# A fused two-block transformer kernel: the in-chunk step sums of the mixer, four heads at a time in two-part products

## The chip, the cores and the metric

The kernel runs on one core of one Trainium2 chip. The metric is the device time of one execution in microseconds (us), which is the time of that one core. The profile is one execution recorded by the hardware profiler. Its five compute rows are PE (TensorE matmuls), PEld (TensorE weight loads), DVE (VectorE), ACT (ScalarE) and POOL (GpSimd); SP is the engine that issues most DMAs.

## The reference, cut to what matters

Two transformer blocks are computed for 256 tokens of width 1024, all in 32-bit floats. The second block has a feed-forward part, a mixer and a second feed-forward part. The mixer runs a state-space branch (16 heads of 64, two groups of eight, chunks of 128 tokens) beside an attention branch. Inside a chunk the state-space branch needs, for every head, the sum of the steps between two positions, and its exponential:

```python
a_cum = jnp.cumsum((dt * A).reshape(b, nc, CHUNK, SSD_GROUPS, SSD_HPG), axis=2)
seg = a_cum[:, :, :, None] - a_cum[:, :, None, :]
causal = jnp.tril(jnp.ones((CHUNK, CHUNK), dtype=bool))[None, None, :, :, None, None]
Lmat = jnp.exp(jnp.where(causal, seg, -jnp.inf)).astype(dtype)
cb = jnp.einsum('bclgn,bcsgn->bclsg', Cc, Bc)
y_diag = jnp.einsum('bclsg,bclsgr,bcsgrp->bclgrp', cb, Lmat, xdt)
```

`dt * A` is the step of one position and head. `seg[l, s]` is the sum of the steps at the positions after `s` up to `l`. 16 heads times two chunks make 32 matrices of 128x128.

## The kernel before, in words

**Products.** Almost every large product runs on TensorE as three matmuls of a reduced 32-bit type, called fp32r in the profile. A weight slab is loaded into a tile `raw`, ACT casts its high part `wh` (line 179, or 183 with a gain), and DVE or, for a list of chosen slabs, POOL forms the low part `wl` (lines 180 and 184). `part` (lines 216 to 221) and `by_feature` (lines 240 to 259) then add high by high, high by low and low by high. A few small products are done in full 32 bits with one matmul call each; the profile shows two MATMUL records for each such call.

**Order of the work.** The program writes out the order of every engine's instructions by hand, and each engine works its own queue strictly in that order. The main line is a row of slab products. Side work is written as generators: `start` puts one into a list, and `tick` (lines 92 to 96), called after each piece of a slab product, moves each generator on when the number that it last yielded has been counted down. So a generator's instructions stand in each queue between those of the main line, at the place of its tick. `take` (lines 191 to 204) prepares up to two slabs ahead of the one in use, with five `raw` buffers and five pairs of `wh` and `wl`; a slab's DMA can be issued by SP only when a `raw` buffer is free, which is when its low part has been formed.

**The mixer (from line 1177).** The first product gives the raw steps and the latent queries (`queries`, line 1217), the second the latent keys and values (`keys`, line 1225, which copies the result out of PSUM on ACT, line 1227), the third the B and C inputs (slabs `X["bc"]`, `by_feature` at line 1277). Meanwhile two sorts of generators run. `latent_chain` (line 1207) normalises and transposes the latents: its transposes are PE instructions at line 272, and they read the copy of line 1227. `steps` (line 1191) forms `dt` and `dA`, the step of every position and head (128x32), by a chain of small DVE instructions (lines 338 to 352, then 1197 and 1198). Its second stage is issued in the same tick as the second stage of the second query chain, whose cast is the ACT instruction of line 266 on a tile of 384 columns.

**The state-space part.** `ssd(g)` (line 1377) is a generator that runs beside the products of the gate slabs `X["z", 0]` and `X["z", 1]`, once for each group of eight heads; `inputs(1, ps)` runs beside the first of them and puts its own POOL work (line 1272) into the same queue. Work is cut into four units of four heads (two chunks by two halves). In step s it issues, in this order: for unit s, on POOL, the product of the strict triangle `after` with the steps of four heads (line 1401, a tile `gm` of 128x512, three buffers); for unit s-2, on PE, four products with the inputs (line 1410) and on DVE their sum (line 1412); for unit s-1, on PE, four 32-bit products with `gm` as stationary operand and the triangle `upper` as moving operand of 128 columns (line 1418), on ACT the exponential back into `gm` (line 1419), and on DVE the product with `cb` (line 1420). Steps 1 and 3 have one more 32-bit product of 512 columns each (lines 1424 and 1429). Two ticks pass between steps. Before step 0, POOL forms `xdd` (line 1384).

Of the kernel before, what the change touches and what calls it, by code (L numbers as in the profile page):

```python
# [10 lines left out]
F32R = mybir.dt.float32r  # L11
I32 = mybir.dt.int32
AF = mybir.ActivationFunctionType
OP = mybir.AluOpType
# [4 lines left out]
H = 16  # L19
NEG = -1e30  # L20
EPS = 1e-6
TP = 128
# [6 lines left out]
def kernel(ctx: ExitStack, tc: tile.TileContext, a: dict, out: bass.AP):  # L29
    nc = tc.nc  # L30
    PE, ACT, DVE, POOL = nc.tensor, nc.scalar, nc.vector, nc.gpsimd
# [23 lines left out]
    def mm_ps(shape=(TP, 512)):  # L55
        return psm.tile(list(shape), F32, tag="mm", name="mm")

    BUFS = {"x": 4, "q": 12, "m": 10, "ra": 3, "rb": 6, "pr": 3, "pT": 4, "gm": 3, "rr": 1}

    def sb(tag, shape=(TP, 512), dt=F32, name=None):  # L60
        return s2.tile(list(shape), dt, tag=tag, name=name or tag, bufs=BUFS[tag])

# [3 lines left out]
    def tt(shape, name="t", dt=F32):  # L66
        return tiny.tile(list(shape), dt, tag="t", name=name)

    def f(ap):
        return ap.bitcast(F32)  # L70
# [193 lines left out]
    def split(hi, lo, src):  # L264

        ACT.copy(hi, src)  # L266
        DVE.tensor_tensor(lo, src, f(hi), op=OP.subtract)  # L267
# [70 lines left out]
    def log1p_of(e, shape):  # L338

        z = tt(shape, "z")  # L340
        q = tt(shape, "q")
        DVE.tensor_scalar(q, e, 2.0, None, op0=OP.add)
        DVE.reciprocal(q, q)
        DVE.tensor_tensor(z, e, q, op=OP.mult)
        DVE.tensor_tensor(q, z, z, op=OP.mult)
        r = tt(shape, "r")
        DVE.tensor_scalar(r, q, 1.0 / 17, None, op0=OP.mult)
        for c in (15, 13, 11, 9, 7, 5, 3):
            DVE.scalar_tensor_tensor(out=r, in0=r, scalar=1.0 / c, in1=q, op0=OP.add, op1=OP.mult)
        DVE.scalar_tensor_tensor(out=r, in0=r, scalar=1.0, in1=z, op0=OP.add, op1=OP.mult)  # L350
        DVE.tensor_scalar(r, r, 2.0, None, op0=OP.mult)
        return r
# [116 lines left out]
    upper = const.tile([TP, TP], F32)  # L469
    POOL.affine_select(out=upper, in_=ones, pattern=[[1, TP]], compare_op=OP.is_ge,  # L470
                       fill=0.0, base=0, channel_multiplier=-1)
    after = const.tile([TP, TP], F32)
# [704 lines left out]
    def mixer(xT, chains, gate, next_chain, between):  # L1177
# [4 lines left out]
        dtr = keep.tile([TP, 2, H], F32, name="dtr")  # L1182
        dt = keep.tile([TP, 2, H], F32, name="dt")
        dA = keep.tile([TP, 2, H], F32, name="dA")
        decay = keep.tile([TP, H], F32, name="decay")
        ea = keep.tile([TP, H], F32, name="ea")
        kr = [keep.tile([TP, 32], F32, name=f"kr{t}") for t in range(2)]
# [3 lines left out]
        def steps():  # L1191
            e = tt((TP, 2, H), "dte")
            DVE.scalar_tensor_tensor(out=e, in0=dtr, scalar=-1.0, in1=dtr, op0=OP.mult, op1=OP.min)
            ACT.activation(out=e, in_=e, func=AF.Exp)
            yield 4
            l1 = log1p_of(e, (TP, 2, H))
            DVE.scalar_tensor_tensor(out=dt, in0=dtr, scalar=0.0, in1=l1, op0=OP.max, op1=OP.add)
            DVE.scalar_tensor_tensor(out=dA, in0=dt, scalar=-1.0, in1=a_bc.unsqueeze(1).to_broadcast([TP, 2, H]),
                                     op0=OP.mult, op1=OP.mult)
            yield 8  # L1200
            p = mm_ps((TP, 2, H))
            PE.matmul(p[:, 0, :], lhsT=after, rhs=dA[:, 0, :], start=True, stop=True)
            PE.matmul(p[:, 1, :], lhsT=upper, rhs=dA[:, 1, :], start=True, stop=True)
            ACT.activation(out=decay, in_=p[:, 0, :], func=AF.Exp)
            ACT.activation(out=ea, in_=p[:, 1, :], func=AF.Exp)
# [89 lines left out]
        for hf in range(2):  # L1295
# [9 lines left out]
            for q in range(2):  # L1305
                ps = [mm_ps((TP, 2, 192)) for _ in range(2)]

                def kv_out(t):
                    ACT.mul(ktok[t][:, 2 * q:2 * q + 2, 0:64], ps[t][:, :, 0:64], rk[t])
                    ACT.mul(vt[t][:, 2 * q:2 * q + 2, :], ps[t][:, :, 64:192], rk[t])  # L1310
                    if q == 1:
# [3 lines left out]
                         after=kv_out)  # L1315
# [61 lines left out]
        def ssd(g):  # L1377
            hs = slice(8 * g, 8 * g + 8)
            p = mm_ps((TP, TP))
            PE.transpose(p, bT[:, g, 0:TP], ident)  # L1380
            bt = cbp.tile([TP, TP], F32, tag="cb", name="bt")
            ACT.copy(bt, p)
            xd = sb("rb", name="xdd")
            POOL.tensor_tensor(by_head(xd), by_head(xdt[0][g]), decay[:, hs].unsqueeze(2).to_broadcast([TP, 8, 64]),
                               op=OP.mult)
            cb = []
            for t in range(2):
                p = mm_ps((TP, TP))
                PE.matmul(p, lhsT=bT[:, g, tok(t)], rhs=cT[:, g, tok(t)], start=True, stop=True)
                x = cbp.tile([TP, TP], F32, tag="cb", name="cb")  # L1390
                DVE.tensor_tensor(x, p, upper, op=OP.mult)
                cb.append(x)
            units = [(t, b) for t in range(2) for b in range(2)]
            ms = {}
            prev = None
            for s in range(len(units) + 2):
                if s < len(units):
                    t, b = units[s]
                    h0 = 8 * g + 4 * b
                    m = sb("gm", (TP, 4, TP))  # L1400
                    POOL.tensor_tensor(m, after.unsqueeze(1).to_broadcast([TP, 4, TP]),
                                       dA[:, t, h0:h0 + 4].unsqueeze(2).to_broadcast([TP, 4, TP]), op=OP.mult)
                    ms[s] = m
                if s >= 2:
                    t, b = units[s - 2]
                    m, y = ms.pop(s - 2), xs_tok[t][g]
                    p = mm_ps((TP, 256))
                    for i in range(4):
                        c0 = (4 * b + i) * 64
                        PE.matmul(p[:, i * 64:(i + 1) * 64], lhsT=m[:, i, :], rhs=xdt[t][g][:, c0:c0 + 64],  # L1410
                                  start=True, stop=True)
                    DVE.tensor_tensor(y[:, b * 256:(b + 1) * 256], y[:, b * 256:(b + 1) * 256], p, op=OP.add)
                if 1 <= s <= len(units):
                    t, b = units[s - 1]
                    m = ms[s - 1]
                    p = mm_ps((TP, 4, TP))
                    for i in range(4):
                        PE.matmul(p[:, i, :], lhsT=m[:, i, :], rhs=upper, start=True, stop=True)
                    ACT.activation(out=m, in_=p, func=AF.Exp)
                    DVE.tensor_tensor(m, m, cb[t].unsqueeze(1).to_broadcast([TP, 4, TP]), op=OP.mult)  # L1420
                if s == 1:

                    p = mm_ps()
                    PE.matmul(p, lhsT=bt, rhs=xd, start=True, stop=True)
                    prev = sb("rb", name="prev")
                    ACT.copy(prev, p)
                if s == 3:
                    p = mm_ps()
                    PE.matmul(p, lhsT=cT[:, g, tok(1)], rhs=prev, start=True, stop=True)
                    yo = sb("ra", (TP, 8, 64), name="yo")  # L1430
                    DVE.tensor_tensor(yo, by_head(p), ea[:, hs].unsqueeze(2).to_broadcast([TP, 8, 64]), op=OP.mult)
                    y = xs_tok[1][g]
                    DVE.tensor_tensor(y, y, yo.rearrange("p h d -> p (h d)"), op=OP.add)
                yield 2
# [80 lines left out]
    keep = const  # L1515
# [136 lines left out]
```

## Time and profile before

| | |
|---|---|
| three runs | 1186.57, 1189.31, 1192.03 us (median 1189.31) |
| the profiled execution | 1188.71 us, of which the traced span is 1187.0 us |
| instructions in the trace | 19943 |
| bytes moved by DMA | 243.04 MB, 205 GB/s in the mean |
| granted TensorE clock, mean | 0.996 of full speed |

The profiled execution is 0.60 us below the median of the runs, and 1.71 us of its time lie outside the span. A row of a timeline gives the start in us from the span's start, the duration, the engine, the line, the operation, the tile written and the tiles read, the shape, and in brackets how long the engine had stood idle and what ended it. A row of a table of windows gives, for a stretch, its length, then each engine's busy time with the instruction count, then the granted TensorE clock as a share of full speed, then the DMA share and rate. The durations of neighbouring matmuls overlap; the spacing of their starts is what a matmul costs in a row of them.

### The profile page before, as it was taken

To read this page: it belongs to the slowest core of one execution; us is meant where nothing else is said; L and a number is where in the kernel's file an instruction comes from. 1 tells how busy PE (TensorE), PEld (TensorE's weight loads), DVE (VectorE), ACT (ScalarE), POOL (GpSimd) and SP (SyncE) were. 2 spreads that over 40 slices of the span, in tenths; PEclk is the share of its full clock that TensorE was granted. 3 is DMA by queue.
4 is the path that set the end of the run, shared out by engine and by line. 5 is a ranking of instruction groups with operands and counts; after the bars stand their busy time and mean duration, and the time that the engine had idled before them with its cause. 6 is when DMAs were issued, how large, how long until landed. Compare 5 with 4: busy or idle time off the path is not lost. (4 is left out here: it accounts for less than half of the span.)

```text
span 1187.0 us, 19943 instructions
## 1 busy us (share of the span) xinstructions
PE 1162.7 (98%) x7669; PEld 1047.6 (88%) x7669; DVE 832.5 (70%) x1187; ACT 673.9 (57%) x1148; POOL 250.8 (21%) x226
## 2 busy tenths in 40 slices
PE   8999999999999999999999999999998999999997
PEld 7987989988898799899878999978987887999996
DVE  5664678886666467788687788766776786766445
ACT  6476675565556675566654444535766573444443
POOL 3044202223003502112002121103147400112001
PEclk9999999999999999999999999999999999999999
DMA  8643567887553348799737978843733273777661
GB/s 270 195 142 107 181 219 262 295 287 223 170 174 123 129 151 282 242 308 318 244 133 256 314 274 303 275 154 101 222 92 107 90 268 125 244 222 246 209 193 38
DMA packets 128479, 243.04 MB, mean 205 GB/s; under 512 B 8515, under 2 KB 16612, under 8 KB 128384
## 3 DMA queue, kind: packets, MB, share of 16 engines
q1 hardware_dynamic: 126688, 239.96, 61.4%
q0 software_dynamic: 1376, 1.28, 0.5%
q8 instruction: 60, 0.98, 0.3%
q10 hardware_dynamic: 320, 0.53, 0.1%
q14 instruction: 35, 0.29, 0.1%
HBM read 240.65 MB, written 1.09 MB: 204 GB/s over the span
## 5 line engine op out<-in xcount | busy, mean ns | idle before, releaser
L179 ACT CAST wh<-raw 128x1024 fp32r<-128x1024 f32 (+1 forms) x231 | 237.4, 1041 | 220.3 <-DMA raw<-in_w_down_dram 64.1
L180 DVE TENSOR_TENSOR wl<-raw,wh 128x1024 fp32r<-128x1024 f32 (+1 forms) x201 | 261.5, 1319 | 128.0 <-ACT wh L179 125.9
L252 PE MATMUL mm<-xh,wh 128*128 128x256 f32 x1088 | 308.5, 284 | 0.0
L254 PE MATMUL mm<-xh,wl 128*128 128x256 f32 x1088 | 307.9, 283 | 0.0
L253 PE MATMUL mm<-xl,wh 128*128 128x256 f32 x1088 | 307.9, 283 | 0.0
L184 DVE SCALAR_TENSOR_TENSOR wl<-raw,cols,wh 128x512 fp32r<-128x512 f32 (+1 forms) x270 | 203.8, 806 | 65.2 <-ACT wh L183 65.1
L219 PE MATMUL acc<-wh,mh 128*128 128x512 f32 x524 | 208.0, 397 | 2.4 <-ACT mh L266 2.4
L183 ACT ACTIVATE wh<-raw,cols 128x512 fp32r<-128x512 f32 (+1 forms) x270 | 176.0, 708 | 59.3 <-PE acc L253 20.1
L253 PEld LDWEIGHTS mm<-xl,wh 128*128 128x128 f32 x1088 | 208.8, 192 | 0.8
L252 PEld LDWEIGHTS mm<-xh,wh 128*128 128x128 f32 x1088 | 208.8, 192 | 0.8
L254 PEld LDWEIGHTS mm<-xh,wl 128*128 128x128 f32 x1088 | 208.7, 192 | 0.0
L221 PE MATMUL acc<-wh,ml 128*128 128x512 f32 x524 | 205.1, 391 | 0.0
L220 PE MATMUL acc<-wl,mh 128*128 128x512 f32 x524 | 204.9, 391 | 0.0
L509 POOL PARTITION_ALL_REDUCE ada<-ada x18 | 64.3, 3572 | 338.2 <-DVE ada L504 140.2
L219 PEld LDWEIGHTS acc<-wh,mh 128*128 128x128 f32 x524 | 98.9, 189 | 24.4 <-ACT mh L266 4.0
L221 PEld LDWEIGHTS acc<-wh,ml 128*128 128x128 f32 x524 | 98.6, 188 | 22.5 <-DVE ml L267 1.5
L220 PEld LDWEIGHTS acc<-wl,mh 128*128 128x128 f32 x524 | 99.0, 189 | 19.1 <-DVE wl L180 0.5
L504 DVE SCALAR_TENSOR_TENSOR ada<-raw,c_act,ada 128x512 f32<-128x512 f32 x144 | 107.8, 748 | 3.5 <-DMA raw<-in_w_ada_dram 1.0
L252 PE MATMUL acc<-xh,wh 128*128 128x256 f32 x352 | 102.0, 290 | 0.0
L253 PE MATMUL acc<-xl,wh 128*128 128x256 f32 x352 | 99.5, 283 | 0.0
L254 PE MATMUL acc<-xh,wl 128*128 128x256 f32 x352 | 99.5, 283 | 0.0
L180 POOL TENSOR_TENSOR wl<-raw,wh 128x1024 fp32r<-128x1024 f32 x30 | 71.8, 2396 | 108.9 <-ACT wh L179 103.7
(320 smaller groups left out, 1602.4 us busy)
## 6 DMA issues: line engine op xcount, KB each, us to landing
raw<-in_w_ada_dram SPq DMA_DIRECT2D x72, 512.0 KB, 5.4
raw<-in_w_up_dram SPq DMA_DIRECT2D x64, 512.0 KB, 4.8
raw<-in_w_down_dram SPq DMA_DIRECT2D x64, 512.0 KB, 5.6
raw<-in_ffn_w_gate_dram SPq DMA_DIRECT2D x44, 512.0 KB, 4.9
raw<-in_ffn_w_up_dram SPq DMA_DIRECT2D x44, 512.0 KB, 4.8
raw<-in_ffn_w_down_dram SPq DMA_DIRECT2D x44, 512.0 KB, 4.8
raw<-in_moba_w_qkv_dram SPq DMA_DIRECT2D x23, 512.0 KB, 5.8
raw<-in_w_in_dram SPq DMA_DIRECT2D x20, 512.0 KB, 4.4
```

The source lines that it names most:

```text
L179: ACT.copy(hi, raw)
L180: (POOL if i in on_pool else DVE).tensor_tensor(lo, raw, f(hi), op=OP.subtract)
L183: ACT.mul(hi[:, k], raw[:, k], gain[k])
L184: DVE.scalar_tensor_tensor(out=lo[:, k], in0=raw[:, k], scalar=gain[k], in1=f(hi[:, k]), op0=OP.mult, op1=OP.subtract)
L219: PE.matmul(p, lhsT=xh, rhs=wh, start=first and n == 0, stop=False)
L220: PE.matmul(p, lhsT=xh, rhs=wl, start=False, stop=False)
L221: PE.matmul(p, lhsT=xl, rhs=wh, start=False, stop=last and n == len(ws) - 1)
L252: PE.matmul(o, lhsT=wh[:, c], rhs=xh, start=k == 0 and n % 2 == 0, stop=False)
L253: PE.matmul(o, lhsT=wh[:, c], rhs=xl, start=False, stop=False)
L254: PE.matmul(o, lhsT=wl[:, c], rhs=xh, start=False, stop=k == 7 and n % 2 == 1)
L504: DVE.scalar_tensor_tensor(out=acc, in0=raw[:, i, :], scalar=c_act[:, k:k + 1], in1=acc, op0=OP.mult, op1=OP.add)
L509: POOL.partition_all_reduce(acc, acc, TP, ReduceOp.add)
```

## The change

`dA` is cut into a high and a low part of the type fp32r when it has been formed (ACT copies, DVE subtracts), and ACT copies the triangle `after` into an fp32r tile `after_r`. In `ssd`, POOL now makes two tiles `gx` for each unit, the triangle `upper` times the high parts and the same times the low parts of the steps of four heads, and PE makes one product of 512 columns with each, with `after_r` as stationary operand, summed in PSUM. Before, it was one call of 128 columns for each head. The POOL instructions now come last in the step. The exponential goes to a tile `gm` of its own, with one buffer; `gx` has two.

```diff
-    BUFS = {"x": 4, "q": 12, "m": 10, "ra": 3, "rb": 6, "pr": 3, "pT": 4, "gm": 3, "rr": 1}
+    BUFS = {"x": 4, "q": 12, "m": 10, "ra": 3, "rb": 6, "pr": 3, "pT": 4, "gm": 1, "gx": 2, "rr": 1}
...
         dA = keep.tile([TP, 2, H], F32, name="dA")
+        dAp = [keep.tile([TP, 2, H], F32R, name=f"dA{x}") for x in "hl"]
+        after_r = keep.tile([TP, TP], F32R, name="after_r")
...
             DVE.scalar_tensor_tensor(out=dA, in0=dt, scalar=-1.0, in1=a_bc.unsqueeze(1).to_broadcast([TP, 2, H]),
                                      op0=OP.mult, op1=OP.mult)
+            split(*dAp, dA)
+            ACT.copy(after_r, after)
             yield 8
...
             for s in range(len(units) + 2):
-                if s < len(units):
-                    t, b = units[s]
-                    h0 = 8 * g + 4 * b
-                    m = sb("gm", (TP, 4, TP))
-                    POOL.tensor_tensor(m, after.unsqueeze(1).to_broadcast([TP, 4, TP]),
-                                       dA[:, t, h0:h0 + 4].unsqueeze(2).to_broadcast([TP, 4, TP]), op=OP.mult)
-                    ms[s] = m
                 if s >= 2:
...
                 if 1 <= s <= len(units):
                     t, b = units[s - 1]
-                    m = ms[s - 1]
                     p = mm_ps((TP, 4, TP))
-                    for i in range(4):
-                        PE.matmul(p[:, i, :], lhsT=m[:, i, :], rhs=upper, start=True, stop=True)
+                    for i, m in enumerate(ms[s - 1]):
+                        PE.matmul(p, lhsT=after_r, rhs=m, start=i == 0, stop=i == 1)
+                    m = ms[s - 1] = sb("gm", (TP, 4, TP))
                     ACT.activation(out=m, in_=p, func=AF.Exp)
                     DVE.tensor_tensor(m, m, cb[t].unsqueeze(1).to_broadcast([TP, 4, TP]), op=OP.mult)
+                if s < len(units):
+                    t, b = units[s]
+                    h0 = 8 * g + 4 * b
+
+                    ms[s] = [sb("gx", (TP, 4, TP), F32R) for _ in range(2)]
+                    for m, d in zip(ms[s], dAp):
+                        POOL.tensor_tensor(m, upper.unsqueeze(1).to_broadcast([TP, 4, TP]),
+                                           f(d)[:, t, h0:h0 + 4].unsqueeze(2).to_broadcast([TP, 4, TP]), op=OP.mult)
                 if s == 1:
```

## Rows read from the trace of the kernel before

**Rows 1.** The page, busy time of each engine over the whole span.
```profile
PE 1162.7 (98%) x7669; PEld 1047.6 (88%) x7669; DVE 832.5 (70%) x1187; ACT 673.9 (57%) x1148; POOL 250.8 (21%) x226
```

**Rows 2.** Windows: ten us in the state-space part.
```profile
920.00:930.00 10.00, 8.84 (x51) 6.87 (x49) 5.16 (x9) 5.25 (x10) 7.35 (x8) 1.00 0.20 56
```

**Rows 3.** Timeline of PE: one unit at line 1418 and the matmuls behind it.
```profile
933.22 1.11 PE L1418 MATMUL mm<-upper,gm 128*128 128x128 f32 x8
934.09 0.48 PE L219 MATMUL acc<-wh,xh 128*128 128x512 f32 x1
934.41 0.39 PE L220 MATMUL acc<-wl,xh 128*128 128x512 f32 x1
934.64 0.39 PE L221 MATMUL acc<-wh,xl 128*128 128x512 f32 x1
```

**Rows 4.** Timeline of ACT, around the second stage of `steps`.
```profile
818.55 0.23 ACT L1194 ACTIVATE dte<-dte 128x32 f32<-128x32 f32 x1 [0.21 <-DVE dte L1193]
...
820.98 1.06 ACT L179 CAST wh<-raw 128x1024 fp32r<-128x1024 f32 x1
822.20 1.05 ACT L179 CAST wh<-raw 128x1024 fp32r<-128x1024 f32 x1 [0.16 <-PE acc L221]
823.15 0.39 ACT L1227 COPY ckv<-acc 128x288 f32<-128x288 f32 x1
```

**Rows 5.** Chain that ended last, in order of time, two links on DVE.
```profile
825.55 2.42 DVE r L349
...
829.58 0.20 DVE dA L1198
```

**Rows 6.** Timeline of POOL beside that chain.
```profile
825.51 2.41 POOL L180 TENSOR_TENSOR wl<-raw,wh 128x1024 fp32r<-128x1024 f32 x1
```

**Rows 7.** Timeline of PE: the transposes that read the copy of line 1227.
```profile
827.91 0.38 PE L272 MATMUL mm<-ident,ckv 128*128 128x128 f32 x2
```

**Rows 8.** Timeline of PE: three places at which it stood for over 1.1 us.
```profile
785.50 0.50 PE L219 MATMUL acc<-wh,mh 128*128 128x512 f32 x1 [1.64 <-ACT mh L266]
...
909.81 1.07 PE L1410 MATMUL mm<-xdt,gm 128*128 128x64 f32 x8 [1.21 <-ACT th L1251]
...
926.67 1.16 PE L1418 MATMUL mm<-upper,gm 128*128 128x128 f32 x8 [1.16 <-POOL gm L1401]
```

**Rows 9.** Windows behind the first and the last of these places.
```profile
786.00:788.00 2.00, 2.00 (x6) 1.18 (x6) 1.31 (x3) 1.20 (x2) 0.00 (x0) 0.80 0.73 264
788.00:790.00 2.00, 2.00 (x6) 1.50 (x5) 1.74 (x3) 2.00 (x3) 0.00 (x0) 0.50 0.02 6
790.00:792.00 2.00, 2.00 (x8) 1.56 (x8) 2.00 (x3) 0.08 (x1) 0.00 (x0) 0.84 0.52 147
...
928.00:932.00 4.00, 4.00 (x21) 2.95 (x20) 3.27 (x7) 2.45 (x4) 0.81 (x1) 1.00 0.00 0
```

**Rows 10.** Groups by line and shape: the POOL product of line 1401.
```profile
L1401 POOL TENSOR_TENSOR gm<-after,dA 128x512 f32<-128x512 f32 x8 | 10.1, 1266 | 4.3 <-PE mm L1410 4.3
```

**Rows 11.** Timeline of POOL in the state-space part.
```profile
902.96 2.37 POOL L180 TENSOR_TENSOR wl<-raw,wh 128x1024 fp32r<-128x1024 f32 x1
...
913.54 2.39 POOL L180 TENSOR_TENSOR wl<-raw,wh 128x1024 fp32r<-128x1024 f32 x1 [5.76 <-ACT wh L179]
...
916.73 1.04 POOL L1272 TENSOR_TENSOR xdt<-xs,dt 128x512 f32<-128x512 f32 x1 [0.80 <-ACT xs L1270]
...
918.86 1.49 POOL L1401 TENSOR_TENSOR gm<-after,dA 128x512 f32<-128x512 f32 x1
...
925.58 2.04 POOL L1401 TENSOR_TENSOR gm<-after,dA 128x512 f32<-128x512 f32 x2
```

**Rows 12.** Timeline of DVE beside these POOL instructions.
```profile
904.01 1.87 DVE L1252 SCALAR_TENSOR_TENSOR xf<-th,xf 128x512 f32<-128x512 f32 x1
...
910.79 0.67 DVE L1252 SCALAR_TENSOR_TENSOR xf<-th,xf 128x512 f32<-128x512 f32 x1
...
918.44 1.01 DVE L1420 TENSOR_TENSOR gm<-gm,cb 128x512 f32<-128x512 f32 x1 [1.21 <-ACT gm L1419]
```

## The prediction

> **What bounds the kernel now.** I began with the busy times of the page. PE is busy 98% of the span [rows 1], so whatever shortens PE's own queue is worth its full length, as long as nothing makes PE stand instead. Then I read the stages that the change touches. In the state-space part PE is not full: in one ten-us window it is busy 8.84, while POOL is busy 7.35 [rows 2]. The timeline of PE shows why. At 926.67 PE had stood 1.16 us for the POOL product of line 1401, and at 909.81 it had stood 1.21 us [rows 8]. So the POOL queue sets the pace at one place of this part, and PE at most others. Last I read the stage where `dA` is formed, on ACT, DVE, POOL and PE, since the change puts ACT instructions there.
>
> **PE's saving.** A unit's four 32-bit products start at 933.22, and the next matmul at 934.09: 0.87 us. The first fp32r matmul behind them is followed after 0.32, the next after 0.23, so 0.09 is paid for changing over [rows 3]. The new pair costs two spacings of 512 columns and the same change-over, 0.23 + 0.32 = 0.55, and the matmul behind it no longer pays its 0.09. That is 0.87 + 0.09 - 0.55 = 0.41 us saved in each of eight units, 3.3 us in all.
>
> **The ACT queue at `steps`.** This is the added wait that matters. The copy of the high part of `dA` enters ACT's queue in the tick of the second stage, ahead of the casts that start at 820.98 and 822.20 and of the copy of line 1227 at 823.15 [rows 4]. But `dA` is ready only at 829.78 [rows 5], so ACT stands with all of these behind the copy. The stand shortens one thing. One link of the DVE chain took 2.42 us instead of 0.20, since POOL's low part of a slab ran from 825.51 to 827.92 and it waited for that [rows 5, 6]. That low part needs the cast of 820.98, which is now held, so it cannot run then and the chain ends 2.2 us earlier, at 827.55. ACT then does the new copy (0.23 for 32 columns by line 1194) and that of the triangle (about 0.25, an estimate between 0.23 for 32 and 0.39 for 288 columns), overlapped to 0.3, then the two casts at the spacing of 0.95, which is 1.06 less the overlap of some 0.1, then the copy of line 1227 in 0.39: 827.55 + 0.3 + 1.9 + 0.4 = 830.15. The transposes at 827.91 read that copy [rows 7], and PE cannot pass them. PE comes 2.25 us later. Its bounds are 0, if the chain's other links end earlier than I think, and 4.5, if the chain gains nothing (829.78 + 2.6 less 827.91). I take 2.3, since the link of 2.42 ends with POOL's instruction to 0.05 us. The held slab's low part ends near 831.4 on POOL, before its product at some 832.7, so it costs nothing. Its `raw` buffer comes free 3.4 us later and SP's next loads with it, against 2.3 of PE; the casts of those slabs follow their loads by more than the 1.1 left over, so nothing waits there. The DVE subtraction of the low part, some 0.2 us, lies in this stand.
>
> **The clock behind that stand.** After PE had stood 1.64 us at 785.50, the granted clock fell to 0.50, which is 1.2 of 2.4 GHz, and the three windows behind it read 0.80, 0.50 and 0.84: 2 x (0.20 + 0.50 + 0.16) = 1.7 us of full clock lost. After 1.16 us at 926.67 it stayed at 1.00 [rows 8, 9]. A stand of 2.3 us is nearer to the first. Bounds 0 and 1.7; I take 1.7.
>
> **POOL's second product.** Line 1401 took 1.27 us in the mean and 1.02 where two ran together in 2.04 [rows 10, 11]. The new product has the same shape, and there are 16 instead of 8, so POOL gets 8.2 to 10.1 us more. Where is it covered? At units 1 to 3 of both groups POOL may start when PE has done the pair before, and two products take 2.0 to 2.5, against 6.5 us from pair to pair (926.67 to 933.22) [rows 3, 8]: covered. Formerly it could run two units ahead; that lead is lost, and what is queued behind unit 2 on POOL, the low part at 913.54, waits with it, but POOL stood 5.76 us before that and has room [rows 11]. There are three places without cover.
> - Unit 0 of the first group. POOL went on to line 180 at 902.96, so a second product ends near 904.0, some 1.0 later. PE can do the first of the pair meanwhile and loses some 0.7 us, which the stand of 1.21 at 909.81 takes up again [rows 8, 11].
> - The low part of line 180 at 902.96 moves back by the same 1.0. DVE's line 1252 at 904.01 took 1.87 us there and ended as POOL's instruction did, against 0.67 at 910.79 [rows 11, 12]. If it again waits for the end, the stand at 909.81 grows by 1.0; if DVE gets in ahead, it shrinks by up to 1.2. The two starts lie within 0.1 us of each other, so I take 0 and keep both ends.
> - Unit 0 of the second group. POOL works without a gap from 916.73 on, and the first of the two products at 925.58 ended near 926.6, when PE's stand ended [rows 8, 11]. Into that stretch go a second product of unit 3 (at 918.86 one took 1.49) and one of unit 0 (1.02): 1.3 (between 1.02 and 1.49) + 1.0 = 2.3 us, less 0.4, since the stretch waits for an ACT copy of PE's transposes [rows 11] and PE has unit 1's saving behind it there. POOL is ready at 926.6 + 1.9 = 928.5; only the pair's second matmul is then left, so PE goes on near 928.8, where before its four calls were done 0.9 after 926.67, near 927.6. It is 1.2 later there, and the stand grows from 1.16 to about 3 us, since PE comes 1.2 earlier with three units saved. Bounds: 0.3 later, if both products take their 1.0 beside idle DVE and the stretch begins a us sooner, and 2.1, if it begins no sooner and the products take 1.5.
>
> The last three units save 3 x 0.41 = 1.2, so this part ends where it did: 0. The long stand has again the clock as its price, 1.7 by the row that it is nearer to [rows 8, 9], with 0 as the other end.
>
> Edits at no cost: the one buffer of `gm`, since the products that read it stand ahead of the pair on PE; and `dA` itself at lines 1202 and 1203, read as before.
>
> **A page beside it.** The row of 904.01 shows DVE held to the end of POOL's instruction; that of 918.44 shows the DVE product at 1.01 and a POOL product of 1.49 beside it, both stretched [rows 11, 12]. The Trainium skill, "SBUF — State Buffer", section "SBUF: two separate sides", says that the two engines' shared ports are an exclusive lock held for the whole instruction. By that rule the 0 of the second place would be 1.0 and the sum that much higher; by the row of 918.44, where both got through in part, it stays.
>
> **The sum.** 2.3 for ACT's queue, 1.7 for the clock, 0 for the state-space part (PE's 3.3 is in it) and 1.7 for the clock again make 5.7 us against the profiled execution's 1188.71: 1194.4. The median of the runs is 0.60 above that execution, well inside their own spread of 5.5, so I leave it at **1194.4 us**.
>
> **The rivals.**
> - *The clock stays up.* The stands come as worked out but no low clock follows either. For it speaks that a stand of 1.21 us brought none; against it the one of 1.64. 1188.71 + 2.3 = 1191.0 us. Chance 0.14.
> - *PE's saving is all that shows (faster).* ACT's copy finds `dA` done, or its held work is not waited for, and POOL's product at the second group stays covered. The places are the transposes at 827.91 and the pair at 926.67; the point from which it decides is whether ACT's copy of line 1227 and POOL's second product end before PE arrives. For it: PE is the bound at 98%. Against it: the order of ACT's queue, which is fixed. 1188.71 - 3.3 = 1185.4 us. Chance 0.14.
> - *DVE is held by POOL (slower still).* The place is line 1252 at 904.01. If DVE waits there for the low part that now ends 1.04 later, PE stands at 909.81 for over 2 us, and pays the clock a third time: 1194.4 + 1.0 + 1.7 = 1197.1 us. It decides if POOL takes up its instruction before DVE does. For it the row of 1.87, against it the row of 1.01. By the lock rule of the Trainium skill's page "SBUF — State Buffer" it would come so. Chance 0.20.
> - *The pair is no faster.* If a 512-column product cost as much with these tiles as a 32-bit call of 512 columns, some 0.87 by the same number of columns in a unit, the unit would cost 1.74: 8 x (1.74 - 0.55) = 9.5 us more than in the sum, 1203.9. Against it: every fp32r matmul of 512 columns beside it is 0.23 from the next [rows 3]. Chance 0.02.
>
> **How the numbers follow.** The forecast has a chance of 0.50, with an own range of 1191.5 to 1196.5: it loses part of a low-clock stretch at the lower end, and takes longer POOL instructions at the upper. A measurement of this kernel can tell about 0.5%, 5.9 us, from no change, so faster means under 1183.4 and slower over 1195.3. Slower gets the whole of the third and fourth rivals and somewhat over a quarter of the forecast: 0.20 + 0.02 + 0.14 = 0.36. Faster needs more than all of PE's saving, so it gets 0.04 out of the second rival, for the spread of the runs. The rest, 0.60, is within. The range of 1187.5 to 1198.5 leaves out most of the second rival (0.10), the top of the third (0.06) and the fourth, together under 0.2.
>
> **What would show it.** In the profile after: on ACT a copy of 32 columns at the place of 821, with an idle time of over 6 us before it that DVE ended; the link of the DVE chain back at 0.20; PE idle for about 2.2 us before the transposes of line 272, and a granted clock of 0.50 in the windows behind; 16 POOL products near 1.04 to 1.3 us each; the pair's spacing 0.55 or less; a stand of over 2 us at the first unit of the second group. I am wrong if PE doesn't stand at the transposes, if the clock stays at 1.00 behind both stands, or if the state-space part as a whole gets longer by more than 2 us at full clock.

## The result and the profile after

The changed kernel takes **1196.3 us** (median of 7 runs, 1192.89 to 1198.66) against 1187.91 for the kernel before (7 runs): a ratio of 1.0070, 95% interval 1.0056 to 1.0084. It is slower by 8.4 us, above the 0.5% that was to be told apart; that class had a chance of 0.36, "within" had 0.60. The time lies in the range, 1.9 us above the forecast. The profiled execution took 1197.49, its span is 1195.8. Lines of the changed kernel have other numbers than before: 1251 is now 1255, 1252 is 1256, 1401 is 1424, 1410 is 1407, 1418 is 1414, 1227 is 1231, 1198 is 1200.

The page, busy times of each engine in the kernel after, answers to [rows 1]:

```profile
PE 1164.7 (97%) x7621; PEld 1045.5 (87%) x7621; DVE 833.9 (70%) x1188; ACT 673.0 (56%) x1150; POOL 260.6 (22%) x234
```

PE has 48 matmuls fewer and yet 2.0 us more busy time; its matmuls at half clock take longer (0.63 for 0.39 at 914.74). To see where the time went I cut the span at three PE instructions that the change doesn't touch. First in the kernel before (timeline of PE):

```profile
810.17 0.45 PE L219 MATMUL acc<-qh,xh 128*128 128x400 f32 x1 [1.00 <-ACT xh L266]
...
898.26 0.49 PE L1389 MATMUL mm<-cT,bT 128*128 128x128 f32 x2 [0.91 <-ACT pT L566]
...
988.74 0.60 PE L272 MATMUL mm<-ident,hn 128*128 128x128 f32 x4
```

Then in the kernel after, the same three and every place of the two stretches that matters (timeline of PE):

```profile
809.85 0.45 PE L219 MATMUL acc<-qh,xh 128*128 128x400 f32 x1 [0.99 <-ACT xh L266]
...
828.31 0.44 PE L272 MATMUL mm<-ident,ckv 128*128 128x128 f32 x2 [2.14 <-ACT ckv L1231]
...
899.87 0.49 PE L1393 MATMUL mm<-cT,bT 128*128 128x128 f32 x2 [0.90 <-ACT pT L566]
...
912.31 1.08 PE L1407 MATMUL mm<-xdt,gm 128*128 128x64 f32 x8 [1.75 <-ACT th L1255]
913.20 0.72 PE L1414 MATMUL mm<-gx,after_r 128*128 128x512 f32 x2
913.75 0.39 PE L219 MATMUL acc<-wh,xh 128*128 128x512 f32 x1
...
931.48 0.80 PE L1414 MATMUL mm<-gx,after_r 128*128 128x512 f32 x1 [3.10 <-POOL gx L1424]
...
950.94 1.10 PE L1407 MATMUL mm<-xdt,gm 128*128 128x64 f32 x8 [0.61 <-DVE gm L1417]
...
955.88 1.08 PE L1407 MATMUL mm<-xdt,gm 128*128 128x64 f32 x8 [0.56 <-DVE gm L1417]
...
996.90 0.60 PE L272 MATMUL mm<-ident,hn 128*128 128x128 f32 x4
```

The first stretch, in which `steps` runs, went from 88.09 us (898.26 - 810.17) to 90.02. The second, the state-space part, went from 90.48 to **97.03**. Of the 8.8 us between the spans, 6.55 are in the part that was forecast to gain nothing at full clock and to pay 1.7 for the clock. The pair itself is what it was costed at: 913.20 to 913.75 is 0.55, against 0.87 in [rows 3].

The granted clock behind the stands (windows of the kernel after; the columns are the window, its length, the busy times of PE, PEld, DVE, ACT and POOL, the clock, the DMA share and GB/s):

```profile
828.00:830.00 2.00, 1.69 (x10) 1.69 (x11) 2.00 (x1) 1.94 (x7) 1.92 (x2) 0.68 0.03 8
830.00:832.00 2.00, 2.00 (x12) 2.00 (x12) 2.00 (x14) 1.47 (x5) 1.75 (x4) 0.50 0.44 132
832.00:834.00 2.00, 2.00 (x18) 2.00 (x17) 2.00 (x5) 1.57 (x5) 1.01 (x3) 0.96 0.80 250
...
914.00:916.00 2.00, 2.00 (x6) 1.54 (x5) 1.49 (x3) 1.48 (x2) 2.00 (x2) 0.52 0.74 207
916.00:918.00 2.00, 2.00 (x11) 1.94 (x10) 0.19 (x1) 0.60 (x1) 2.00 (x2) 0.63 0.15 55
...
930.00:932.00 2.00, 0.52 (x1) 0.29 (x1) 0.00 (x0) 0.79 (x2) 2.00 (x3) 0.78 0.23 87
932.00:934.00 2.00, 1.80 (x5) 0.91 (x4) 0.00 (x0) 0.00 (x0) 2.00 (x3) 0.50 0.03 8
934.00:936.00 2.00, 2.00 (x5) 1.25 (x4) 0.98 (x3) 0.00 (x0) 0.42 (x1) 0.50 0.00 0
936.00:938.00 2.00, 2.00 (x8) 1.65 (x7) 1.56 (x3) 0.00 (x0) 0.00 (x0) 0.51 0.00 0
```

With the loss of a window as 2 us times what the clock lacks of 1.00, as the prediction reckoned [rows 9], the three stretches at half clock (1.2 of 2.4 GHz) lose 1.72, 1.70 and 3.42 us. The last is an upper bound, since part of it ran while PE stood.

ACT's queue in the kernel after (timeline of ACT), to be held against [rows 4]:

```profile
825.65 0.22 ACT L266 CAST dAh<-dA 128x32 fp32r<-128x32 f32 x1 [6.47 <-DVE dA L1200]
825.78 0.29 ACT L1203 CAST after_r<-after 128x128 fp32r<-128x128 f32 x1
825.98 1.99 ACT L179 CAST wh<-raw 128x1024 fp32r<-128x1024 f32 x2
827.87 0.39 ACT L1231 COPY ckv<-acc 128x288 f32<-128x288 f32 x1
```

ACT stands 6.47 us for `dA`, then does the two copies and two casts before the copy for which PE has stood 2.14 us. DVE's chain is quicker for it, as forecast: its seven steps at line 349 now take 1.55 us together, where one link alone took 2.42 [rows 5] (timeline of DVE):

```profile
823.17 1.55 DVE L349 SCALAR_TENSOR_TENSOR r<-r,q 128x32 f32<-128x32 f32 x7
...
905.62 2.76 DVE L1256 SCALAR_TENSOR_TENSOR xf<-th,xf 128x512 f32<-128x512 f32 x1
...
913.29 0.67 DVE L1256 SCALAR_TENSOR_TENSOR xf<-th,xf 128x512 f32<-128x512 f32 x1
...
947.27 2.08 DVE L184 SCALAR_TENSOR_TENSOR wl<-raw,cols,wh 128x512 fp32r<-128x512 f32 x2
```

POOL beside it in the state-space part (timeline of POOL), and the low-part product over its eight instructions (the view of line 1424: shortest, median and longest in ns, first and last start):

```profile
903.46 1.04 POOL L1424 TENSOR_TENSOR gx<-upper,dAh 128x512 fp32r<-128x512 f32 x1
904.46 1.04 POOL L1424 TENSOR_TENSOR gx<-upper,dAl 128x512 fp32r<-128x512 f32 x1
905.46 2.38 POOL L180 TENSOR_TENSOR wl<-raw,wh 128x1024 fp32r<-128x1024 f32 x1
...
929.39 1.04 POOL L1388 TENSOR_TENSOR xdd<-xdt,decay 128x512 f32<-128x512 f32 x1
930.39 1.04 POOL L1424 TENSOR_TENSOR gx<-upper,dAh 128x512 fp32r<-128x512 f32 x1
931.38 1.04 POOL L1424 TENSOR_TENSOR gx<-upper,dAl 128x512 fp32r<-128x512 f32 x1
```

```profile
L1424 POOL TENSOR_TENSOR gx<-upper,dAl x8: 1037/1040/1567, 904.5 to 947.1; 128x512 fp32r<-128x512 f32 x8
```

Three things are to be seen. The second product starts at 904.46, the low part of line 180 follows at 905.46 and ends at 907.84, and DVE's line 1256, begun at 905.62, ends at 908.38: 2.76 us where it took 1.87 [rows 12]. PE's stand of 3.10 ends when POOL's first product of the second group does, and a second one follows. And late in the part, at 947.27, a pair of DVE's slab steps takes 2.08 us beside the last low-part product of POOL, which starts at 947.1; PE then stands 0.61 at 950.94 and 0.56 at 955.88 for DVE's `gm`, at places where the kernel before had no stand of over 0.5 us.

### The profile page after: what moved, and what is told of

Same layout as the page of the kernel before. It is cut to its first block, busy times and chain, and to the rows that moved or that the text cites. A ratio compares the mean times of both kernels' runs of the same rounds, so it can differ in the third digit from the quotient of the medians.

```text
span 1195.8 us, 19862 instructions
## 1 busy us (share of the span) xinstructions
PE 1164.7 (97%) x7621; PEld 1045.5 (87%) x7621; DVE 833.9 (70%) x1188; ACT 673.0 (56%) x1150; POOL 260.6 (22%) x234
## 5 line engine op out<-in xcount | busy, mean ns | idle before, releaser
L509 POOL PARTITION_ALL_REDUCE ada<-ada x18 | 66.7, 3707 | 339.0 <-DVE ada L504 140.2
```

Of the source, the lines that this page charges most:

```text
L509: POOL.partition_all_reduce(acc, acc, TP, ReduceOp.add)
```

## The experiments

Each of the twelve kernels was timed against the kernel before on the same chip. The ratios stand as recorded, with their intervals; the ratio of two medians of the table can differ from them by up to 0.07%. The two stretches are cut in each profile as above; "loss" is the sum of 2 us x (1 - granted clock) over the 2-us windows of the state-space part, and the last column is what is left without it. One profile of each kernel stands behind the four right-hand columns, so they show mechanisms; the ratios are the times.

| kernel | median us | ratio (95%) | first stretch | state space | loss | without |
|---|---|---|---|---|---|---|
| before | 1187.3 to 1188.3 | 1 | 88.09 | 90.48 | 0 | 90.48 |
| after | 1196.30 | 1.0070 (1.0056-1.0084) | 90.02 | 97.03 | 5.12 | 91.91 |
| e1 split late | 1191.28 | 1.0039 (1.0025-1.0053) | 86.46 | 94.45 | 1.72 | 92.73 |
| e2 split only | 1190.82 | 1.0033 (1.0021-1.0045) | 90.03 | 90.49 | 0 | 90.49 |
| e3 one POOL product | 1191.62 | 1.0036 (1.0024-1.0049) | 91.52 | 90.27 | 1.72 | 88.55 |
| e4 = e1 + e3 | 1187.64 | 1.0001 (0.9992-1.0010) | 86.49 | 90.26 | 1.72 | 88.54 |
| e5 = e1 + DVE | 1189.91 | 1.0012 (1.0003-1.0021) | 86.51 | 94.64 | 3.42 | 91.22 |
| e6 = e5 + early | 1189.00 | 1.0012 (1.0002-1.0022) | 88.06 | 92.13 | 1.70 | 90.43 |
| e7 = e6 + 4th `cb` | 1189.93 | 1.0020 (1.0008-1.0032) | 87.93 | 93.88 | 3.42 | 90.46 |
| e8 = e7 + `prev` later | 1191.35 | 1.0031 (1.0017-1.0045) | 87.86 | 94.59 | 5.12 | 89.47 |
| e9 = e6 + `xdd` sooner | 1188.09 | 1.0002 (0.9991-1.0014) | 88.06 | 90.83 | 0 | 90.83 |
| e10 = e9 + `gm` on POOL | 1187.52 | 0.9999 (0.9988-1.0011) | 88.13 | 89.27 | 0 | 89.27 |
| e11 = before + two moves | 1186.29 | 0.9987 (0.9976-0.9998) | 86.54 | 89.19 | 0 | 89.19 |
| e12 = e1 + `xdd` sooner | 1191.78 | 1.0033 (1.0020-1.0046) | 86.52 | 94.79 | 1.70 | 93.09 |

The first stretch carries 1.7 us of low clock where it reads 88 (after the first cut, as in the kernel before, where the windows from 810 to 816 read 0.78, 0.50 and 0.87), the same behind the stand at `ckv` in the kernel after and e2, both in e3, and none where it reads 86.5.

**e1 to e4: which half costs what.**

e1 moves the split behind the exponentials that follow it:

```diff
-            split(*dAp, dA)
-            ACT.copy(after_r, after)
             yield 8
 ...
             ACT.activation(out=ea, in_=p[:, 1, :], func=AF.Exp)
+            split(*dAp, dA)
+            ACT.copy(after_r, after)
```

> The changed kernel with one part moved: the two ACT copies and the DVE subtraction that form dAh, dAl and after_r are issued after the exponentials that give decay and ea, so that ACT no longer waits for dA with the casts and the copy of ckv behind it. Theory (two separate losses, ACT's queue and POOL's second product): the stand of 2.1 us before the transposes of ckv and the low clock behind it go, the state-space part stays as it is with its stands of 1.75 and 3.1 us: about 1196.3 - 2.1 - 1.7 = 1192.5 us. Rival (the state-space part alone costs the time, a PE stand before it is made up later by the stands there): no change, 1195 to 1197 us.

e2 is the kernel before with these two lines (and the tiles that they write) at the place of the change, read by nobody:

> The kernel before with one part of the change alone: dAh, dAl and after_r are formed at the place where the change forms them, and nothing reads them; POOL and PE work as before. Theory: ACT waits some 6.5 us for dA, PE stands some 2.1 us at the transposes of ckv and loses 1.7 us more by a low clock: 1187.9 + 3.8 = 1191.7 us, and the state-space part as in the kernel before. Rival (the split is hidden): 1188 us.

e3 is the changed kernel with one POOL product per unit, that of the high parts, which both products of PE read (the low parts are left out), and e4 is e3 with e1's move:

```diff
-                    ms[s] = [sb("gx", (TP, 4, TP), F32R) for _ in range(2)]
-                    for m, d in zip(ms[s], dAp):
+                    ms[s] = [sb("gx", (TP, 4, TP), F32R)] * 2
+                    for m, d in zip(ms[s][:1], dAp):
```

> The changed kernel with the low part left out: POOL forms one tile gx for each unit, from the high parts of the steps, and both 512-column products of PE read it; the low part of the steps is left out of the sums and the high part is counted twice. POOL has as many products as before, PE as many as after. Theory: the stand at the first unit of the second group falls from 3.1 to about 2 us, that at the first product of the first group to about 1.2, so the state-space part loses at most one low-clock stretch, and PE's saving of about 2 us shows; ACT's queue costs 3.8 as before: 1187.9 + 3.8 - 2 + 1 = 1190.7 us, the DVE instruction that was held for 2.76 us back at 1.9 or less. Rival (POOL's second product is covered, and ACT's queue alone costs the time): 1195 to 1197 us.

> Both edits together: the split issued late, and one POOL product for each unit from the high parts, read by both products of PE; the low part is left out of the sums and the high part counted twice. Theory: neither loss is left, PE's saving shows in part: 1187.9 - 2 + 1 = 1187 us (1184.6 if all of it shows). Rival (PE's products of 512 columns are what costs the time, by their own length): above 1192 us.

All four came out on the theory's side, 0.6 to 1.2 us from its times. The two halves add up. The split's place costs 0.33% by e2, 0.31% by after less e1 and 0.35% by e3 less e4, 3.7 to 4.2 us; the second product costs 0.34% by after less e3 and 0.38% by e1 less e4, 4.0 to 4.5. With both gone, PE's saving leaves e4 level with the kernel before. In e1 the places that the next paragraphs refer to are these (timeline of PE):

```profile
896.12 0.49 PE L1393 MATMUL mm<-cT,bT 128*128 128x128 f32 x2 [0.90 <-ACT pT L566]
...
908.58 1.08 PE L1407 MATMUL mm<-xdt,gm 128*128 128x64 f32 x8 [1.76 <-ACT th L1255]
...
926.12 0.50 PE L1414 MATMUL mm<-gx,after_r 128*128 128x512 f32 x1 [3.07 <-POOL gx L1424]
...
927.12 0.50 PE L1414 MATMUL mm<-gx,after_r 128*128 128x512 f32 x1 [0.50 <-POOL gx L1424]
```

In e2 the stand has the length that it has in the kernel after (timeline of PE):

```profile
829.03 0.44 PE L272 MATMUL mm<-ident,ckv 128*128 128x128 f32 x2 [2.14 <-ACT ckv L1231]
```

and the whole of it is in the first stretch: e2's state-space part is that of the kernel before to 0.01 us. e4 shows where PE's saving goes (timeline of PE):

```profile
907.30 1.08 PE L1407 MATMUL mm<-xdt,gm 128*128 128x64 f32 x8 [1.67 <-ACT th L1255]
...
923.73 0.72 PE L1414 MATMUL mm<-gx,after_r 128*128 128x512 f32 x2 [1.97 <-POOL gx L1424]
```

The two stands of the kernel before, 1.21 and 1.16 [rows 8], have grown by 0.46 and 0.81, since PE comes sooner to things that come when they came. Of 3.3 us saved 2.0 are left, which is the 1.94 that e4 is shorter without loss, and a low clock behind the longer stand takes 1.72 of them.

**e5 to e8: moving the second product out of POOL's way.**

e5 and e6 form the pair's operands in a helper, on a given engine:

```diff
+            done = True            # e5: g == 1
+            ms = {0: parts((1, 0, 0), DVE) if g == 1 else first}    # e5: empty for g == 0
 ...
-                    ms[s] = [sb("gx", (TP, 4, TP), F32R) for _ in range(2)]
 ...
+                    if s or not done:
+                        ms[s] = parts((g, t, b), POOL)
 ...
         finish(*latent)
+        first = parts((0, 0, 0), POOL)     # from e6 on
```

> The split stands behind the exponentials, as in e1 (1191.3 us), and besides the two products of the first unit of the second group are made on DVE ahead of its two cb products, where DVE idles from about 927 to 935 us in the changed kernel; all other units keep theirs on POOL. Theory (in e1 the stand of 3.07 us ahead of that unit, and the low clock behind it, is the price of the second POOL product in POOL's queue behind xdt, xs, v, y and xdd): the two products end some 3 us sooner than on POOL, the stand falls to 1.2 us or less, and the time is 1191.3 - 1.9 (stand) - 1.7 (half of 3.4 us at the low clock) = 1187.7 us; 1186 if the stand goes altogether. Rival (the stand is not POOL's doing but that of data that come late, xdd or cb among them): it stays at 2.5 us or more, and 1190.5 to 1192 us. Second rival (DVE and POOL exclude each other, so what DVE makes there makes POOL's xdt and xs later): the stand moves to the second unit, 1189 to 1191.

> As e5, and the two products of the first unit of the first group are made on POOL as soon as the steps are there (behind the products of bc, when POOL has nothing to do), in place of 903 us, where they keep the moved slab low part of 2.4 us, and with it DVE's convolution step, waiting. Theory (the stand of 1.75 us at the first products of xs, and the low clock behind it, come from that queue): POOL starts the slab part 2 us sooner, DVE's step is no longer held to 2.8 us, the stand falls to 0.8 us or less: 1.0 below e5, and 1.7 more where e5 had a low clock there, so about 1186.7, down to 1185. Rival (the stand is set by the convolution's own chain, with POOL beside it without effect): within 0.5 us of e5.

e5 gained 0.27% on e1. Its time is in the second rival's range, by another way: the stand of 3.07 falls to 0.67, but the next work in PE's queue then stands 1.25 us for `xdd`, which POOL still forms behind `xs`, `v` and `y`. The theory's 1187.7 was missed by 2.2 us. e6's two products are gone from POOL at that place, and DVE's step is short again (timeline of DVE in e6):

```profile
903.79 1.90 DVE L1256 SCALAR_TENSOR_TENSOR xf<-th,xf 128x512 f32<-128x512 f32 x1
...
910.59 0.67 DVE L1256 SCALAR_TENSOR_TENSOR xf<-th,xf 128x512 f32<-128x512 f32 x1
```

but PE's stand there is not (timeline of PE in e6):

```profile
909.61 1.08 PE L1419 MATMUL mm<-xdt,gm 128*128 128x64 f32 x8 [1.70 <-ACT th L1255]
...
926.99 2.08 PE L1437 MATMUL mm<-xdd,bt 128*128 128x512 f32 x2 [1.25 <-POOL xdd L1400]
```

The length of a stand misleads here, and the moment at which it ends does not. Counted from the second cut, PE goes on after 11.55 us in the kernel before (909.81 - 898.26) and after 11.56 to 11.59 in e2, e3, e4 and e6 to e9. In the four kernels with two products ahead of POOL's slab part (after, e1, e5, e12) it goes on after 12.44 to 12.47. The step is 0.89, and DVE's instruction is 2.76 or 2.77 instead of 1.87 to 1.91 in just these four: 0.86 to 0.90. So the second product does hold DVE, and by DVE's queue PE; without it PE merely waits for the moment that held before. The ratio doesn't tell e6 from e5 (1.0012 both; the medians are 0.9 us apart), so the time went to e6's rival and not to its theory (1186.7), though the part without loss is 0.8 us shorter.

```diff
-    cbp = pool("cbp", 3)
+    cbp = pool("cbp", 4)           # e7
 ...
-                if s == 1:
+                if s == 2:             # e8
```

> As e6, with a fourth buffer for the tiles bt and cb, so that DVE's second cb product of the second group no longer waits for the product that reads bt (idle time of 4.7 us in the kernel before, 7.4 in the changed one). Theory (the wait ends before its result is wanted by more than a unit, DVE's other work behind it has slack): within 0.5 us of e6. Rival (DVE's gate products stand in its queue behind it, and the two late stands of 0.6 us are its doing): 1.2 us below e6.

> As e7, and the product of bt with xdd (and the copy of prev) is issued one step later, when xdd (POOL) has long been written. Theory: PE's queue no longer holds behind xdd, worth at most 0.5 us where the stand ahead of that unit's products is the one that counts: e7 - 0.5 to e7. Rival (prev is then late for the last step of the group, which reads it): e7 + 0.5 to + 1.5.

e7's theory held for the mechanism: without loss 90.46 against 90.43, and the two late stands of about 0.6 us are still there (0.63 and 0.56), so the wait for the `cb` buffer is off the path. Its ratio is 0.08% above e6's, inside the intervals. e8 is 0.11% above e7, in its rival's range, by another way than the rival's. With the product of `bt` moved behind, PE has that much less to do ahead of the first stand; the moment stays (11.59), the stand grows to 2.59 us, and behind it 3.40 us are lost at half clock in this profile; 1.72 more are lost behind a stand of 1.50 at 934.62. At full clock the part is 1.0 us shorter than e7's, so here it is the low clock that costs the time.

**e9 to e12: the two queues.**

```diff
                 for o, w in ((y, dt[...]), (x, ds_bc[...])):
                     POOL.tensor_tensor(by_head(o), by_head(x), ..., op=OP.mult)
+                    if t == 0 and g == 1 and o is y:
+                        xds.append(sb("rb", name="xdd"))
+                        POOL.tensor_tensor(by_head(xds[0]), by_head(y), decay[...], op=OP.mult)
 ...
-                    DVE.tensor_tensor(m, m, cb[t]..., op=OP.mult)
+                    (POOL if g == 0 and s == 1 else DVE).tensor_tensor(m, m, cb[t]..., op=OP.mult)
```

The first hunk is in e9 to e12 (in the second group `ssd` then takes that `xdd` and forms none), the second in e10 and e11.

> As e6 (1189.0 us), and the second group's xdd is formed on POOL straight behind the first xdt it reads, where e6 forms it behind xdt, xs, v and y at 925.9 us, with PE standing 1.25 us for it and 3 to 4 us at half clock behind. Theory (with the two products on DVE, xdd's place in POOL's queue is what PE waits for): the stand of 1.25 us goes, and the half clock behind it may: 1189.0 - 1.25 = 1187.7 us, down to 1186.0 without the low clock. Rival (POOL's queue as a whole is late there, so that the work moved back is waited for instead): a stand of over 1 us stays at the next unit, within 0.5 us of e6.

> As e9, and the product of gm with cb of the first unit of the first group is made on POOL in place of DVE. The stand of 1.7 us ahead of that unit's products with xdt was there with two POOL products ahead of it (1.76), with one (1.67) and with none (1.70), so POOL's products don't set it. Theory (gm's product stands in DVE's queue behind two groups of convolution steps: Exp done at 905.7, product at 908.8): on POOL, idle from 907.6 us, it ends about 0.9 us sooner, and the stand falls to about 0.8 us: 0.9 us below e9, and 1.7 more where a low clock followed. Rival (the products wait for the convolution's own chain by th, which the profile names): the stand stays, within 0.5 us of e9.

> The kernel before, with the two moves of e10 that it can take: the second group's xdd behind the first xdt, and the first unit's gm product on POOL. It has the 32-bit products and neither pair nor parts. The stands of 1.21 and 1.16 us of the kernel before are at these places. Theory (both are set by these two queues in it as well): both fall by 0.8 to 1.0 us, 1188.3 - 1.8 = 1186.5 us; e10 is below it by what is left of PE's 3.3 us, 0.5 to 2 us. Rival (what e10 gains is all in the two moves, the pair is worth nothing beside): e11 within 0.5 us of e10, or below.

> The changed kernel with the split behind the exponentials (e1, 1191.3 us) and the second group's xdd behind the first xdt; both products of every unit stay on POOL. Theory (POOL's queue decides, each of its 1.0 us instructions ahead of the first products of that group counts): e1's stand of 3.07 us falls to about 2.0, 1190.2 us, down to 1188.5 if the low clock goes. Rival (what POOL does ahead is only shifted, since the xdd is in the queue all the same, earlier): within 0.5 us of e1.

e9 came near its theory (0.10% below e6; the stand for `xdd` is gone, and 0.89 us for DVE's product stand in its place, with no low clock in this part of the profile). e10 shows what the profile's "th" hid. With `gm` on POOL, PE doesn't stand at that place (timeline of POOL, then of PE, in e10):

```profile
905.71 1.30 POOL L1437 TENSOR_TENSOR gm<-gm,cb 128x512 f32<-128x512 f32 x1 [0.63 <-ACT gm L1436]
```

```profile
907.23 0.60 PE L272 MATMUL mm<-ident,ym 128*128 128x128 f32 x4
907.66 1.00 PE L1427 MATMUL mm<-xdt,gm 128*128 128x64 f32 x8
```

`th` starts at 908.90 in e10, after PE has gone on, so the wait was for `gm`, held in DVE's queue by the convolution steps ahead of it (in e8 the profile names DVE's `gm` there). e10's part without loss is 1.56 us shorter than e9's; the gain in time, 0.03% by the ratios, is inside the intervals, so the theory's mechanism came and its 0.9 us can't be seen in the time. e11 decides what the pair is worth: the kernel before with the same two moves has the same state-space part, 89.19 against 89.27, with all of PE's 32-bit products in it. Its theory had the time (1186.5) but not both reasons, since the first stand went and the second stayed (timeline of PE in e11):

```profile
924.01 1.16 PE L1426 MATMUL mm<-upper,gm 128*128 128x128 f32 x8 [1.30 <-POOL gm L1409]
```

Nor is e10 below it by 0.5 to 2 us, as that theory had it: the rival came, by which the pair is worth nothing beside the two moves. Its ratio is the lowest of the table, 0.9987, and the only one whose interval lies below 1; e10's interval overlaps it, so the two can't be told apart. e12 went to its rival: the `xdd` moved forward lies in POOL's queue all the same, and e1's long stand of 3.07 us is 2.75. The stand is shorter only because PE comes later, behind 1.70 us lost at half clock: it ends 31.77 us after the second cut, against 30.00 in e1.

## Why the forecast was near, and what failed in it

- **PE's saving, 0.41 us a unit: right**, 0.55 for the pair and 0.23 to the next.
- **ACT's queue, 2.3 us: right.** The stand is 2.14, with the idle time of over 6 us and the short DVE chain that were to show it. By moments, the transposes of `ckv` start 18.46 us after the first cut in the kernel after and 16.16 in e1, where no low clock lies before them: 2.30. The first stretch without its clock loss is 88.30 in the kernel after, 86.39 before: 1.9 us are left of it.
- **The clock behind it, 1.7 us: right** in the profile (1.72), and e2 has it too. But the execution from which the forecast was reckoned had itself lost 1.72 us behind the stand at 785.50 and 1.70 behind the first cut, and the profiles of the kernel after and of e2 lost neither, so between profiles the first stretch grows by 1.9 us alone. That the term comes on top is shown by the runs: e2's 3.9 us (0.33%) are close to 2.3 + 1.7, and its mean granted clock over six runs is 0.9958 against 0.9971 over the 16 runs before beside it, some 1.5 us (an estimate, from clocks of three digits).
- **The second place, taken as 0, was 0.89.** This step failed. I weighed two ends, DVE held to POOL's end (+1.0) or in ahead of it, and let a nearby row of partial overlap decide. DVE's instruction ends 0.54 to 0.55 us behind the end of POOL's slab part in all fourteen profiles, whether POOL still had 1.3 to 1.4 us to run or 2.2 when it began; alone it takes 0.67. So it got almost nothing done beside POOL. The Trainium skill ("SBUF — State Buffer", section "SBUF: two separate sides") calls the shared ports an exclusive lock, held for the whole instruction; these rows agree with it at this place.
- **The state-space part at full clock, 0, was about 2.25** (e1, 92.73 against 90.48; the kernel after's own profile gives at least 1.43, 91.91). By e1 one of the prediction's signs of being wrong came, more than 2 us at full clock. The long stand came as worked out, 3.07 in e1. Its second POOL product ended later than reckoned: counted from the second cut, the second matmul starts 31.00 us on (927.12 - 896.12), where 928.5 would have been 30.24. The 0.76 answers to the 0.89 of the second place, handed on: ACT's copy of `xs`, for which POOL's stretch waits, starts 18.28 us after the cut in e1 and 17.41 in e4, where DVE was held 0.88 less. And "the last three units save 1.2" did not hold: the stands of 0.61 and 0.56 took 1.17 of it back. These stands come with the second product and not with the single `gm` buffer, since e3 and e4 have that buffer, one product, and neither stand (of the kernels with two products e8 alone is without them). I had covered these units for POOL and PE, and not asked what POOL's added products do to DVE's steps beside them: the pair of slab steps at 947.27 took 2.08 us, in e4 1.42. That this is the way by which the stands arise is argued from such rows and not tested by itself.
- **The clock in this part, 1.7, was 5.12** in the profile of the kernel after and 1.72 in that of e1. A second stretch came behind the stand of 1.75, and the one behind the long stand lasted twice as long. The third rival had the first of these, with its price of 1.7 (for a stand that it put at over 2 us), but not the second. The seven runs bear the size out: their mean granted clock is 0.993 against 0.997 of the 16 runs before beside e1 to e4, some 4.7 us (an estimate as above) where the sum had 3.4. With 1.9 us for the first stretch at full clock and 1.4 to 2.25 for the second that makes 8.0 to 8.9; measured are 8.4.

So the forecast of +5.7 had the ACT half right and took the POOL half at 1.7, where e1 against the kernel before shows 0.39%, 4.6 us. The third rival's mechanism, with DVE held, is the one that came; its 1197.1 is 0.8 above the median. That the forecast lies only 1.9 us below the measured time is in part luck: the change was 8.4 us and not 5.7, and 0.8 of the gap is closed because the forecast starts from an execution at 1188.71 where the median of the kernel before is 1187.91. The chances failed in one respect: the bound of 1195.3 for "slower" went by the median of three runs, 1189.31. By that of seven it is 1193.9, below the forecast itself, so 0.60 for "within" was too much.

Left open is why the half clock comes behind a stand in one execution and not in another, and whether the pair could gain anything in an order of work written for it: in e10, which has the shortest state-space part of the kernels with both products, PE still stands 0.94, 0.76, 0.62 and 0.57 us for POOL and DVE.

## What to carry to other kernels

An engine that is busy 98% over a span can be the waiting one in the stage that a change touches, and what is saved on it there only lengthens its next stand; ask what ends each stand, and compare the moments at which stands end, not their lengths. When work is added to an engine with room, follow its queue to the next long instruction beside which another engine has work, and price that as a full hold until a row says otherwise; here 1.0 us more on POOL held DVE 0.86 to 0.90 us longer. A copy that waits for a late value belongs behind the work that doesn't need it: moving two lines was worth 3.7 us by the ratios (0.31%).

## What the runs showed of the hardware

In the part between 780 and 1000 us the half clock came in stretches of one size: each lost 1.70 to 1.72 us, two together 3.40 or 3.42. A stand's length alone doesn't decide. Behind the stand at the `mh` matmuls near 785 us, ahead of the first cut [rows 8, 9], the clock fell after 1.64 us in the kernel before and 1.59 in e10, and stayed up after 1.73 in e1; in the state-space part it fell after 1.75 in the kernel after and stayed up after 1.76 in e1. The spread between runs of one kernel goes with the clock: of 33 runs of the kernel before beside e9 to e12, the 23 with a mean granted clock of 0.998 took 1187.3 us in the mean, the 7 with 0.995 took 1189.9. A sum over stands should therefore have each stretch as a term of 0 or 1.7, and not as a sure one, with 3.4 as its upper end: that much was lost at the stands of 3.10 us in the kernel after, 2.59 in e8 and 1.72 in e7.
